# A hybrid decoder block on one core: the whole program's order written out, output weights split once, layer norms in one chain, two FFN pairs by turns, operands at multiples of 512 bytes

## The chip, the cores and the metric

The kernel runs on one core of one Trainium2 chip. The metric is the time of one execution on the device in microseconds (us). A profile of one execution records what each engine did: TensorE (PE, its weight loads as PEld), VectorE (DVE), ScalarE (ACT), GpSimd (POOL) and the sync engine (SP), which here only issues transfers (DMAs).

## The reference

One block over 16 learned tokens and 1024 tokens of width 1024, in float32. `D_FF` is 2816; `W_A = W_B = 512`.

```python
h = concat(meta, x)
xn = rms_norm(h, pre_mix_norm)
b_gate, c_gate, h_a, glu_val, glu_gate = split(xn @ w_in, 512 each)
y_a = b_gate * causal_conv3(c_gate * h_a)
g   = glu_val * sigmoid(glu_gate)
z   = causal_conv31(g) + conv_b_bias
y_b = silu(layer_norm(z, ln_b_gain, ln_b_bias))
h = h + rms_norm(concat(y_a, y_b) @ w_out, post_mix_norm)
n = rms_norm(h, pre_ffn_norm)
ff = (silu(n @ w_gate) * (n @ w_up)) @ w_down
out = (h + rms_norm(ff, post_ffn_norm))[16:]
```

## The kernel before

**Precision.** Each operand of a matmul is split into a high part (rounded to the matmul's type) and a low part (what is left); `mm3` multiplies high by high, high by low and low by high into one PSUM bank. So each product is three matmuls, and each operand needs a copy on ACT (high) and a subtraction on DVE or POOL (low).

**Input projection.** Channels lie on partitions, tokens along them. There are 20 units of 128 output channels: four each of g (gate of the gated group), v (its value), c, h and b (the short convolution group). g and v run over 1044 columns (4 of padding, 16 learned tokens, 1024 tokens) in three parts of 348, c and h over 1026 in three parts of 342, b over 1024 in two parts of 512; every part is summed over eight blocks k of the input. A unit's result takes three PSUM banks (`ps1`, two tiles, so the next unit but one waits for a unit's result to be read). Units g0 and v0 run together while the input arrives; then the sum of squares for the first norm (`ss_x`), its reciprocal root (`rsqrt_n`, on DVE), and its spread over partitions (`pb_x`, `rB`).

**Long convolution.** 31 taps over even and odd positions apart, after an identity that shares 16 taps: `ac` on the odd stream, then `ae` on the difference `d` and `ao` on the shifted difference. Each tap is one DVE instruction of 512 columns that multiplies and adds to an accumulator in a PSUM bank (`aux`, two banks). The first eight shared taps of groups 1 to 3 are done on ACT and POOL (`conv_head`). The 163 taps left for DVE were issued with low priority (`later()`).

**Layer norm.** One call for each half of the positions: sum over channels (`chunk_sum`, a matmul with `ones`), subtraction of the mean, squares, a second sum, root, spread by transposes, scale, SiLU, split. The first half was called behind unit b1, the second behind b3.

**Output projection.** Row blocks of 128 tokens in groups of three, three and two; each group runs over eight blocks of `w_out`, which each group loaded and split anew (24 splits). Then two RMS norms with the residual (`norms`), and `turn` transposes the result (`pt`, `aux` banks) into `raw`.

**FFN.** One level of Strassen's scheme in Winograd's form, seven products. For gate and up it runs over 11 pairs of blocks of `D_FF` (`Pair`), whose weights are the stationary operands (`op`) and whose seven moving operands are B11, B21, B22 and T1 to T4, sums of the transposed input's quarters (`X`). A product is 24 matmuls of 512 columns. The results are combined, split and written to DRAM (`gd`); the down projection reads them back (`a`), with `w_down`'s combinations as moving operands (`db`).

**Order.** Up to the end of the output projection a planner ordered each engine's instructions from a model of their times; from the FFN on, the program's text is the order (`manual_schedule`), and each engine takes its instructions in that order.

**Where tiles lie.** Pools are stacked from the low end of SBUF, some (`side="right"`) from the high end. `xg` holds the input's parts in the first stage and later the FFN's operands, in tiles of `lines(2 * TT)` = 2096 elements, 8384 bytes; `bp` and `rp` hold further operands of 8192 bytes, `wp` weights and operands of 4096.

Of the kernel before, what the change touches and what calls it, by code (L numbers as in the profile page):

```python
# [36 lines left out]
LOW = 2000  # L37
# [9 lines left out]
LINE = 16  # L47

# [6 lines left out]
def hybrid_block(ctx: ExitStack, tc: tile.TileContext, xT, x, w_in, w_out, w_gate, w_up, w_down, par, g_post, g_ffn, g_out, out):  # L55
# [21 lines left out]
    pr = const.tile([P, lines(NPAR)], F32, name="pr")[:, :NPAR]  # L77

    def big(name, dt=F32R, pool=None):

        if pool is None:
            return xg.tile([P, lines(2 * TT)], dt, tag="x", name=name)[:, : 2 * TT]
        return pool.tile([P, 4 * HALF], dt, tag="x", name=name)

    def row(pool, tag, name, n, dt=F32, **k):
        return pool.tile([P, lines(n)], dt, tag=tag, name=name, **k)[:, :n]
# [3 lines left out]

    def load_unit(src, name):
        ws = wp.tile([P, D], F32, tag="ws", name=f"ws_{name}", bufs=3)
        nc.sync.dma_start(ws, src)
        return ws

    def split_unit(ws, name, eng=None):
        wh = wp.tile([P, D], F32R, tag="wh", name=f"wh_{name}")
        wl = wp.tile([P, D], F32R, tag="wl", name=f"wl_{name}")
        nc.scalar.copy(wh, ws)  # L99
        (eng or nc.gpsimd).tensor_tensor(wl, ws, wh.bitcast(F32), op=ALU.subtract)  # L100
        return wh, wl

    def unit(src, name, eng=None):
        return split_unit(load_unit(src, name), name, eng)
# [47 lines left out]
    xl = [xlb[k // 2][:, k % 2, :] for k in range(KD)]

    def load_x(k):
        t = row(tp, "t", f"xs{k}", TT)[:, PAD:]
        nc.sync.dma_start(t, xT[k])
        return t

    w0 = {}
    for n in ("g0", "v0"):  # L160
        w0[n] = [wp.tile([P, D], dt, tag=tag, name=f"{tag}_in_{n}", bufs=3) for dt, tag in ((F32, "ws"), (F32R, "wh"), (F32R, "wl"))]

    def load_w0(n, m, c):
        nc.sync.dma_start(w0[n][0][:, c], units_in(m)[:, c])

    def split_w0(n, c):
        ws, wh, wl = w0[n]
        nc.scalar.copy(wh[:, c], ws[:, c])
        nc.vector.tensor_tensor(wl[:, c], ws[:, c], wh[:, c].bitcast(F32), op=ALU.subtract)

    sa = [row(gp, "g", f"sa{j}", G0 + TT)[:, G0 + PAD :] for j in range(2)]

    def split_x(k):
        h, l, t = xh[k][:, PAD:], xl[k][:, PAD:], xs[k]
        g = pr[:, O_MIX + k : O_MIX + k + 1]
        nc.scalar.activation(h, t, AF.Copy, scale=g)
        nc.vector.scalar_tensor_tensor(l, t, g, h.bitcast(F32), op0=ALU.mult, op1=ALU.subtract)

    def square_x(k):
        t = xs[k]  # L180
        if k < 2:
# [6 lines left out]
    xs = {}
    cut = [slice(0, 2 * P), slice(2 * P, D)]
    for j in range(2):  # L190
        load_w0("g0", M_G, cut[j])
        xs[j] = load_x(j)
        load_w0("v0", M_V, cut[j])
    for k in range(2, KD):
        xs[k] = load_x(k)
    for j in range(2):
        split_w0("g0", cut[j])
        split_x(j)
        split_w0("v0", cut[j])
    for k in range(KD):  # L200
        if k >= 2:
            split_x(k)
# [23 lines left out]
    sx = sm.tile([P, 16], F32, tag="sx", name="sx")  # L226
    nc.gpsimd.memset(sx, 1.0)
# [879 lines left out]
```

## Time and profile before

| | |
|---|---|
| median of three runs | 1053.48 us (1051.01 to 1054.18) |
| the profiled execution, its own time | 1052.19 us |
| its span, first to last instruction | 1050.4 us |
| granted TensorE clock, mean | 0.977 |
| busy: PE, DVE, ACT, POOL | 992.3, 782.9, 396.3, 296.7 us |
| moved by DMAs | 161.93 MB |

The page gives busy times by engine, the span in 40 slices of 26.3 us, the chain of work that ended last, and groups of instructions by line, engine and tile with the time their engine stood idle before them and what ended that. Answers from the trace give who waited for whom, busy times in any stretch, and single instructions. In a row of stages the columns are: stretch, length, busy time and count of PE, PEld, DVE, ACT and POOL, granted clock, busy share of the DMA engines, GB/s. In a row of waits they are: who, for whom, total us, times, longest.

### The profile page before, as it was taken

The page shows a single profiled execution, that of the slowest core. Times are in us where ns is not written, and L with a number is a line of the kernel's source. Part 1 is how long each engine was busy: PE and PEld are TensorE (multiplying, and loading weights), DVE is VectorE, ACT ScalarE, POOL GpSimd, SP SyncE. Part 2 cuts the span into 40 slices and gives each one's busy share as a digit, 9 for nine tenths or more (in the row PEclk, how much of TensorE's full clock was granted, in tenths as well). Part 3 has the DMA queues.
Part 4 walks back from the last instruction along what each step waited for, and adds up shares of the span by engine and source line. Part 5 has one row for each costly group of instructions (what it writes and reads, how often), then busy time and mean ns, then how long its engine had stood idle before and what let it go on. Part 6 is the DMA issues. An engine that isn't in the chain of part 4 may idle for free.

```text
span 1050.4 us, 12734 instructions
## 1 busy us (share of the span) xinstructions
PE 992.3 (94%) x4643; PEld 837.0 (80%) x4643; DVE 782.9 (75%) x1106; ACT 396.3 (38%) x640; POOL 296.7 (28%) x241
## 2 busy tenths in 40 slices
PE   8999899997799977999999999999999999999994
PEld 8998899986588765778888888888888788888773
DVE  6488778999556978788888878879877343446677
ACT  7432142333345554334425324334334233322331
POOL 4464575440000000543413313313312521221110
PEclk9999999999899989999999999999999999999997
DMA  7111111103246550254354344345217989856765
GB/s 286 44 42 37 61 41 41 47 34 100 81 161 222 190 184 5 80 182 153 125 203 157 118 166 168 121 152 183 116 63 256 330 297 379 261 180 212 267 211 211
DMA packets 59727, 161.93 MB, mean 154 GB/s; under 512 B 6289, under 2 KB 6673, under 8 KB 59665
## 3 DMA queue, kind: packets, MB, share of 16 engines
q1 hardware_dynamic: 43056, 108.35, 28.7%
q0 software_dynamic: 11088, 40.38, 12.0%
q10 hardware_dynamic: 5520, 12.40, 3.3%
q8 instruction: 36, 0.59, 0.2%
q14 instruction: 27, 0.21, 0.1%
HBM read 112.34 MB, written 48.76 MB: 153 GB/s over the span
## 4 chain that ended last, share of the span: by engine, by line
PE 61%; DVE 25%; POOL 4%; issue 4%; ACT 4%; DMA 2%; DVEq 0%; ACTq 0%; SPq 0%; POOLq 0%
PE x L108 6%; PE x L109 6%; PE x L110 6%; PE y L110 5%; PE y L109 5%; PE y L108 5%; DVE ae L300 4%; DVE ao L300 3%; PE qx L109 3%; PE qx L108 3%; PE qx L110 3%; PE po L108 3%; PE po L109 3%; PE po L110 3%; PE qy L109 3%
## 5 line engine op out<-in xcount | busy, mean ns | idle before, releaser
L544 DVE TENSOR_TENSOR op<-u,op 128x512 fp32r<-128x512 f32 x132 | 114.5, 892 | 50.4 <-ACT op L555 50.4
L555 ACT CAST op<-u 128x512 fp32r<-128x512 f32 x132 | 78.0, 617 | 154.6 <-DVE u L544 140.3
L544 DVE TENSOR_TENSOR db<-wb,db 128x512 fp32r<-128x512 f32 x77 | 54.9, 716 | 92.7 <-ACT db L912 92.4
L547 POOL TENSOR_TENSOR C<-C,C 128x512 f32<-128x512 f32 x11 | 16.9, 1539 | 344.6 <-ACT C L665 232.3
L912 ACT CAST db<-wb 128x512 fp32r<-128x512 f32 x77 | 47.2, 620 | 125.3 <-PE qx L110 59.8
L108 PE MATMUL qx<-db,a 128*128 128x512 f32 x176 | 69.4, 394 | 2.0 <-DMA a<-gdA 2.0
L109 PE MATMUL qx<-db,a 128*128 128x512 f32 x176 | 69.5, 395 | 0.4 <-DVE db L544 0.3
L110 PE MATMUL qx<-db,a 128*128 128x512 f32 x176 | 69.1, 392 | 0.0
L547 POOL TENSOR_TENSOR U<-U,U 128x512 f32<-128x512 f32 x22 | 31.6, 1435 | 114.4 <-ACT U L665 82.2
L541 DVE TENSOR_TENSOR U<-y,U 128x512 f32<-128x512 f32 x66 | 43.0, 681 | 17.6 <-PE y L110 17.6
L108 PE MATMUL qy<-db,a 128*128 128x512 f32 x132 | 51.5, 390 | 0.5 <-ACT db L912 0.5
L109 PE MATMUL qy<-db,a 128*128 128x512 f32 x132 | 51.5, 390 | 0.3 <-DVE db L544 0.3
L110 PE MATMUL qy<-db,a 128*128 128x512 f32 x132 | 51.4, 389 | 0.0
L888 POOL DMA_DIRECT2D a<-gdS x44 | 23.3, 531 | 92.5 <-PE qy L110 47.2
L100 DVE TENSOR_TENSOR wl_o<-ws_o,wh_o 128x1024 fp32r<-128x1024 f32 x24 | 30.7, 1284 | 22.5 <-ACT wh_o L99 22.3
L99 ACT CAST wh_o<-ws_o 128x1024 fp32r<-128x1024 f32 x24 | 25.2, 1052 | 49.2 <-PE po L110 36.3
L300 DVE SCALAR_TENSOR_TENSOR ae<-d,pr,ae 128x512 f32<-128x512 f32 x56 | 41.1, 749 | 0.4
L108 PEld LDWEIGHTS qx<-db,a 128*128 128x128 f32 x176 | 33.4, 190 | 9.8 <-issue 2.4
L109 PEld LDWEIGHTS qx<-db,a 128*128 128x128 f32 x176 | 33.4, 190 | 8.1 <-DVE db L544 1.2
L108 PE MATMUL y<-T2h,op 128*128 128x512 f32 x88 | 35.5, 404 | 4.1 <-DVE G L547 4.1
L110 PEld LDWEIGHTS qx<-db,a 128*128 128x128 f32 x176 | 33.5, 190 | 7.1
L108 PE MATMUL x<-B11h,op 128*128 128x512 f32 x88 | 35.4, 403 | 2.9 <-ACT op L555 2.9
(307 smaller groups left out, 3099.9 us busy)
## 6 DMA issues: line engine op xcount, KB each, us to landing
a<-gdS POOLq DMA_DIRECT2D x44, 512.0 KB, 4.7
a<-gdA POOLq DMA_DIRECT2D x33, 512.0 KB, 5.6
ws_o<-w_out_u SPq DMA_DIRECT2D x24, 512.0 KB, 3.5
u<-w_gate_u SPq DMA_DIRECT2D x22, 512.0 KB, 5.0
u<-w_up_u SPq DMA_DIRECT2D x22, 512.0 KB, 6.0
gdS<-HI SPq DMA_DIRECT2D x44, 256.0 KB, 2.3
gdA<-HI SPq DMA_DIRECT2D x33, 256.0 KB, 2.0
gdS<-GS SPq DMA_DIRECT2D x33, 256.0 KB, 2.7
```

Source lines behind the costliest of these rows:

```text
L99: nc.scalar.copy(wh, ws)
L100: (eng or nc.gpsimd).tensor_tensor(wl, ws, wh.bitcast(F32), op=ALU.subtract)
L108: nc.tensor.matmul(o, lh, rh, start=start, stop=False, skip_group_check=again)
L109: nc.tensor.matmul(o, lh, rl, start=False, stop=False, skip_group_check=again)
L110: nc.tensor.matmul(o, ll, rh, start=False, stop=stop, skip_group_check=again)
L300: nc.vector.scalar_tensor_tensor(out if i == n - 1 else acc, src[:, i : i + HALF], w(i), init if i == first else acc, op0=ALU.mult, op1=AL ...
L541: (eng or nc.vector).tensor_tensor(o, a, b, op=ALU.add)
L544: (eng or nc.vector).tensor_tensor(o, a, b, op=ALU.subtract)
L547: (eng or nc.vector).tensor_tensor(o, a, b, op=ALU.mult)
L555: nc.scalar.copy(t[:, 0, :], src)
L888: nc.gpsimd.dma_start(loads[n, j], gd[an][j])
L912: nc.scalar.copy(t[:, 0, :], b)
```

## The change

- **Order.** `manual_schedule` now begins at the top. The input projection is a loop over `UNITS`: in each round the next unit's weights are split, those of the unit after it loaded, the last unit's result is read (`after`), and a fixed number of convolution taps is issued (`LEAD_IN`). Small matmuls stand at fixed places between the blocks of a unit (`AT`).
- **Taps.** `by_turns` issues the taps of two chains alternately; chains `common(0)` and `common(3)` run alone.
- **Layer norm.** Both halves go through one chain: `ln_sum` behind the last tap, `ln_mean` behind the first block of b2, `ln_var` and `ln_spread` within c3, `ln_apply` ahead of h3. The splits of `y_b` follow b3.
- **Output weights.** `pre_out` splits each block of `w_out` once, during g0 to g1, and stores both parts in DRAM (`wo`); `load_o` loads them on POOL's queue, 18 times 1 MB, the middle group running its blocks backwards. Three blocks fit.
- **Output projection to FFN.** The transposes of a group's rows stand among the matmuls of the next group, those of 3 to 5 ahead of the last two blocks of the third. Products 1 of pairs 0 and 1 follow that group at once; the norms of rows 6 and 7 run beside them.
- **First pairs.** Pairs 0 and 1 take each product in turn (before: product 1 and 2 of both, then the rest of pair 0, then of pair 1); their splits come together later.
- **Addresses.** `xg` is a pool of its own for the FFN with tiles of 8192 bytes; a pool `fill` of 160 bytes and a wider `edge` shift the pools, so that `bp`, `xg` and `rp` start at multiples of 512 bytes. The input's parts have their own pool `xa`.
- **Smaller.** Two sums of squares go from POOL to DVE, the last group's tail of the short convolution wholly to DVE; combination 6 of a pair is done in place, part of it at product 7.

```diff
-    edge.tile([P, 8], F32, name="edge")
+    edge.tile([P, 120], F32, name="edge")
-    xg = ctx.enter_context(tc.tile_pool(name="xg", bufs=8))
+    fill = ctx.enter_context(tc.tile_pool(name="fill", bufs=1))
+    fill.tile([P, FILL], F32, name="fill")
+    bp = ctx.enter_context(tc.tile_pool(name="bp", bufs=2))
...
+    order_ = ExitStack()
+    order_.enter_context(tc.manual_schedule())
...
-        if pool is None:
-            return xg.tile([P, lines(2 * TT)], dt, tag="x", name=name)[:, : 2 * TT]
-        return pool.tile([P, 4 * HALF], dt, tag="x", name=name)
+        return (pool or xg).tile([P, 4 * HALF], dt, tag="x", name=name)
...
+    def pre_out(k):
+        load_raw_o(k + 2)
+        ws = ws_o.pop(k)
+        h, l = (yap.tile([P, D], F32R, tag="y", name=f"{c}_o{k}") for c in ("wh", "wl"))
+        nc.scalar.copy(h, ws)
+        nc.vector.tensor_tensor(l, ws, h.bitcast(F32), op=ALU.subtract)
+        for q, t in enumerate((h, l)):
+            nc.sync.dma_start(wo[k][:, q, :].bitcast(F32), t.bitcast(F32))
...
+    def conv():
+        yield from common(0)
+        yield from by_turns(even(0), odd(0))
+        yield from by_turns(common(1), common(2))
+        yield from by_turns(even(1), odd(1))
+        yield from by_turns(even(2), odd(2))
+        yield from common(3)
+        yield from by_turns(even(3), odd(3))
...
+    def after_b(a):
+        yh[a], yl[a] = (yap.tile([P, SEQ], F32R, tag="y", name=f"y{c}{a}") for c in "hl")
+        for q in range(2):
+            s = slice(q * HALF, (q + 1) * HALF)
+            nc.vector.tensor_tensor(cv[a][:, s], pu["b", a][:, q, :], cv[a][:, s], op=ALU.mult)
+        nc.scalar.copy(yh[a], cv[a])
+        nc.vector.tensor_tensor(yl[a], cv[a], yh[a].bitcast(F32), op=ALU.subtract)
...
+    def start_g():
+        spread_x()
+        nc.vector.tensor_tensor(sg[0], sg[0], rB, op=ALU.mult)
+        nc.scalar.activation(sg[0], sg[0], AF.Sigmoid)
+        pre_out(6)
+        nc.vector.tensor_tensor(sg[0], sg[0], rB, op=ALU.mult)
+        pre_out(7)
+        o3 = new_g(0)
+        nc.vector.tensor_tensor(o3.rearrange("p r n -> p n r"), vs.rearrange("p (n r) -> p n r", r=2), sg[0].rearrange("p (n r) -> p n r", r=2), op=ALU.mult)
...
+    LEAD_IN = {0: lambda: pre(range(2, 6)), 1: some(lambda: conv_head(0), lambda: tap(9)), 2: some(lambda: conv_head(1), lambda: tap(10)), 3: lambda: tap(14), 4: some(lambda: conv_head(2), lambda: tap(13)), 5: lambda: tap(14), 6: some(lambda: conv_head(3), lambda: tap(12)), 7: lambda: tap(16), 8: lambda: tap(13), 9: lambda: tap(12), 10: lambda: tap(15), 11: lambda: tap(12), 12: lambda: tap(12), 13: some(lambda: tap(40), ln_sum), 16: some(ln_apply), 17: some(gains)}
+    AT = {(0, 1): start_g, (14, 1): ln_mean, (15, 3): ln_var, (15, 7): ln_spread}
+
+    for i, u in enumerate(UNITS):
+        if i + 1 < len(UNITS):
+            split_unit(UNITS[i + 1])
+        if i + 2 < len(UNITS):
+            load_unit(UNITS[i + 2])
+        if i:
+            after[UNITS[i - 1][0]](UNITS[i - 1][1])
+        LEAD_IN.get(i, lambda: None)()
+        p = pu[u] = ps1.tile([P, 3, 512], F32, tag="p", name=f"p_{u[0]}{u[1]}")
+        for k in range(KD):
+            AT.get((i, k), lambda: None)()
+            mm_k(p, split_w[u], k, *GEO[u[0]])
...
-            w = unit(w_out[k], f"o{grp[0]}_{k}", nc.vector)
...
+    def load_o(k):
+        wu[k] = [wp.tile([P, D], F32R, tag=t, name=f"{t}_o{k}") for t in ("wh", "wl")]
+        for q in range(2):
+            nc.gpsimd.dma_start(wu[k][q], wo[k][:, q, :])
+
+    todo_o = list(range(KD)) + list(range(KD - 4, -1, -1)) + list(range(3, KD))
...
+    s1, left = group((3, 4, 5), down_, {4: turns(0, 1), 5: turns(2)})
...
+    s1, left = group((6, 7), up, {6: early})
...
+    results = {s: pairs[order[s][0]].product(order[s][1], made.pop(s)) for s in range(2)}
...
-    order = [(j, n) for n in (1, 2) for j in range(2)] + [(j, n) for j in range(2) for n in (6, 5, 7, 3, 4)]
+    order = [(j, n) for n in (1, 2, 6, 5, 7, 3, 4) for j in range(2)]
...
+    extra = {2: (load_pair(1, 1),), 3: (t2,), 4: (t1,), 6: (t3,), 8: (b22,), 9: (load_pair(2, 0),), 10: (t4,), 11: (load_pair(2, 1),)}
+    first_splits = {13: (0, "A12", "S3"), 14: (0, "S1", "A11"), 15: (0, "A22", "S2", "S4"), 16: (1, "A22", "S3", "S1"), 17: (1, "A11", "S2"), 18: (1, "A12"), 19: (1, "S4")}
```

More of the change, by code (lines that the diff above doesn't have):

```diff
@@ L152, in hybrid_block @@
[L152 to L169, printed above, removed]
@@ L188, in hybrid_block @@
[L188 to L193, printed above, removed]
-    for k in range(2, KD):
[L195 to L202, printed above, removed]
+    sx = sm.tile([P, 16], F32, tag="sx", name="sx")
+    nc.gpsimd.memset(sx, 1.0)
+    wv = pr[:, O_CB : O_CB + 4 * CB].rearrange("p (a j) -> p a j", a=4)
@@ new lines, in value @@
+    def value(a):
+        o4 = new_g(a).rearrange("p r (a n) -> p a n r", a=3)
+        for i in range(3):
+            nc.vector.tensor_tensor(o4[:, i], pu["v", a][:, i, :T3].rearrange("p (n r) -> p n r", r=2), three(sg[a])[:, i].rearrange("p (n r) -> p n r", r=2), op=ALU.mult)
+    sg[0] = row(tp, "t", "sg0", TT)
+    vs = row(tp, "t", "vs0", TT)
+    nc.scalar.copy(three(sg[0]), pu["g", 0][:, :, :T3])
+    nc.scalar.copy(three(vs), pu["v", 0][:, :, :T3])
+    zt = [bp.tile([P, 2, SEQ], F32, tag="x", name=f"z{a}") for a in range(2)]
@@ L363, in later @@
-    def later():
-        return tc.high_priority(offset=-LOW)
-    glu(0, pg0, lambda: pv0, True)
-    with later():
-        conv_head(0)
-    todo_in = [(M_G + a // 2 if a % 2 == 0 else M_V + a // 2, f"in_{'gv'[a % 2]}{a // 2}") for a in range(2, 8)]
-    todo_in += [(m + a, f"in_{c}{a}") for a in range(4) for m, c in ((M_C, "c"), (M_H, "h"), (M_B, "b"))]
-    ahead = []
-    def prepare(n):
-        while len(ahead) < n and todo_in:
-            m, name = todo_in.pop(0)
-            ahead.append((name, unit(units_in(m), name)))
@@ L406, in hybrid_block, with tap @@
+    conv_taps = conv()
+    def tap(n):
+        for i in range(n):
+            next(conv_taps, None)
+    yh, yl = [None] * 8, [None] * 8
     T0 = PAD + META
@@ new lines, in hybrid_block, with sums @@
+    after = {"g": gate, "v": value, "c": after_c, "h": after_h, "b": after_b}
+    GEO = {"g": (0, T3, 3), "v": (0, T3, 3), "c": (T0 - CA + 1, C3, 3), "h": (T0 - CA + 1, C3, 3), "b": (T0, HALF, 2)}
+    LN = [(hf, a) for hf in range(2) for a in range(4)]
+    hs_ = [slice(hf * HALF, (hf + 1) * HALF) for hf in range(2)]
+    ln = {}
+    def sums(srcs, outs):
+        for q in range(3):
+            for hf in range(2):
+                nc.vector.tensor_tensor(outs[hf], srcs(hf, 0) if q == 0 else outs[hf], srcs(hf, q + 1), op=ALU.add)
@@ new lines, in ln_sum, with ln_mean @@
+    def ln_sum():
+        ln["zs"] = [ct.tile([P, HALF], F32, tag="ct", name=f"zs{hf}") for hf in range(2)]
+        sums(lambda hf, a: z[a][:, hs_[hf]], ln["zs"])
+    def ln_mean():
+        ln["pm"] = [aux.tile([P, 512], F32, tag="a", name=f"pm{hf}") for hf in range(2)]
+        for hf in range(2):
+            nc.tensor.matmul(ln["pm"][hf], ones, ln["zs"][hf], start=True, stop=True)
+        t = [row(gp, "g", f"sq{a}", G0 + TT) for a in range(4)]
+        ln["sq"] = {(hf, a): t[a][:, hs_[hf]] for hf, a in LN}
+        for hf, a in LN:
+            nc.vector.tensor_tensor(z[a][:, hs_[hf]], z[a][:, hs_[hf]], ln["pm"][hf], op=ALU.subtract)
+            nc.scalar.activation(ln["sq"][hf, a], z[a][:, hs_[hf]], AF.Square)
+        sums(lambda hf, a: ln["sq"][hf, a], [ln["sq"][hf, 0] for hf in range(2)])
@@ L759, in hybrid_block @@
     st = ctx.enter_context(tc.tile_pool(name="st", bufs=11, reuse_waits="tile"))
-    psf = None
-    last = None
+    a_side(3)
+    for i in range(2):
+        t2_sum(i)
     def t2():
```

588 lines of the change are left out of this document (306 added, 282 removed).

## The prediction

> **What bounds the kernel now.** I read the page first (busy shares, the slices, the chain), then who TensorE waited for, then busy time by stage; for the parts the chain's pieces and single groups.
>
> ```profile
> span 1050.4 us, 12734 instructions
> PE 992.3 (94%) x4643; PEld 837.0 (80%) x4643; DVE 782.9 (75%) x1106; ACT 396.3 (38%) x640; POOL 296.7 (28%) x241
> PE   8999899997799977999999999999999999999994
> DVE  6488778999556978788888878879877343446677
> PEclk9999999999899989999999999999999999999997
> PE 61%; DVE 25%; POOL 4%; issue 4%; ACT 4%; DMA 2%; DVEq 0%; ACTq 0%; SPq 0%; POOLq 0%
> ```
>
> TensorE is 94% busy, so only its holes and its pace can give anything. The holes are in slices 10-11 and 14-15, where the granted clock drops too. The busiest helper there is VectorE, at 9 from slice 7 to 9. By stage (us, then busy time and instruction count of PE, PEld, DVE, ACT, POOL, then clock, DMA share, GB/s), and a row of the chain:
>
> ```profile
> 52.50:78.80 26.30, 26.30 (x167) 26.30 (x167) 22.29 (x22) 9.32 (x12) 17.61 (x12) 1.00 0.13 43
> ...
> 58.00:253.00 195.00, 187.11 (x1075) 177.20 (x1073) 172.66 (x224) 65.01 (x76) 99.03 (x50) 0.98 0.15 49
> 253.00:290.00 37.00, 24.65 (x94) 19.05 (x93) 23.92 (x41) 14.12 (x19) 0.00 (x0) 0.79 0.21 72
> 290.00:360.00 70.00, 70.00 (x315) 57.49 (x314) 48.78 (x91) 36.23 (x64) 0.00 (x0) 0.99 0.56 196
> 360.00:420.00 60.00, 46.43 (x198) 36.23 (x197) 48.98 (x83) 29.76 (x52) 0.00 (x0) 0.91 0.30 105
> 420.00:470.00 50.00, 46.56 (x199) 36.60 (x198) 40.69 (x49) 18.55 (x30) 23.98 (x15) 1.00 0.34 120
> 470.00:814.00 344.00, 344.00 (x1486) 278.28 (x1485) 285.81 (x357) 134.86 (x242) 98.90 (x63) 1.00 0.42 154
> 814.00:840.00 26.00, 23.97 (x99) 19.18 (x98) 9.77 (x12) 7.07 (x11) 13.72 (x16) 0.93 0.93 329
> ...
> 329.10 0.87 PE pt L501 x8
> ```
>
> The paces come from stretches without a hole: 26.30/167 = 0.1575 us for a matmul of 348 or 342 columns, 344/1486 = 0.2315 us for one of 512. Time minus count times pace is what a stage lost. From 58 to 253 us: 192 matmuls of 512 columns (the four b units) and 883 short ones make 183.5, so 11.5 us lost. From 253 to 290: 94 make 21.5, 15.5 lost. From 290 to 360: nothing. From 360 to 420: 158 of 512 and 40 transposes (eight take 0.87) make 41, 19 lost. From 420 to 470: 199 make 46, 4 lost. Around 820: 3.4 lost. Who ended the longest of these waits:
>
> ```profile
> PE po L108 <- DVE cv L428: 6.2, 1, 6.2
> PE pb_r L329 <- DVE s_ln L130: 5.7, 2, 3.3
> PE y L108 <- DVE G L547: 4.1, 1, 4.1
> PE pt L501 <- ACT raw L503: 2.2, 3, 1.7
> ```
>
> VectorE ends most of them: the convolution and the two layer norms at the change from input to output projection, then the combinations of the FFN's first products.
>
> **The change, part by part.** The reference execution is the profiled one: 1052.19 us, 1.8 more than its span and 1.3 under the median of 1053.48.
>
> *1. Input projection, convolution, layer norm.* The removed planner put taps where DVE was free; the listing now gives DVE a fixed queue, and the next unit but one of TensorE waits for each unit's `after` in that queue. Two taps by turns cost less than one chain:
>
> ```profile
> 130.45 6.67 DVE L300 SCALAR_TENSOR_TENSOR ae<-d,pr,ae 128x512 f32<-128x512 f32 x10
> 140.14 6.29 DVE L300 SCALAR_TENSOR_TENSOR ae<-d,pr,ae 128x512 f32<-128x512 f32 x8
> ...
> 32.59 1.81 PE ss_x L225 x18
> 53.54 4.28 DVE g L263
> 259.51 0.76 PE po L108
> ...
> L268 DVE TENSOR_TENSOR g<-p_in_v,sg 128x348 f32<-128x348 f32 x9 | 6.9, 762 | 0.0
> L307 DVE TENSOR_TENSOR d<-g 128x527 f32<-128x527 f32 x4 | 5.0, 1249 | 14.3 <-POOL z L295 14.3
> L313 DVE TENSOR_TENSOR g<-g 128x526 f32<-128x526 f32 x4 | 7.3, 1815 | 0.0
> L300 DVE SCALAR_TENSOR_TENSOR ac<-g,wsum,z 128x512 f32<-128x512 f32 x4 | 6.0, 1497 | 0.9 <-ACT z L291 0.9
> L300 DVE SCALAR_TENSOR_TENSOR ae<-d,pr,z 128x512 f32<-128x512 f32 x4 | 4.8, 1212 | 0.1
> L321 DVE TENSOR_TENSOR zs<-z,z 128x512 f32<-128x512 f32 x2 | 3.6, 1778 | 1.2 <-POOL z L295 1.2
> L428 DVE TENSOR_TENSOR cv<-p_in_b,cv 128x1024 f32<-128x1024 f32 x4 | 4.9, 1219 | 3.0 <-POOL cv L425 3.0
> L100 DVE TENSOR_TENSOR wl_o<-ws_o,wh_o 128x1024 fp32r<-128x1024 f32 x24 | 30.7, 1284 | 22.5 <-ACT wh_o L99 22.3
> L295 POOL TENSOR_TENSOR z<-z,ct 128x512 f32<-128x512 f32 x21 | 29.6, 1409 | 18.8 <-ACT ct L294 18.0
> ```
>
> Ten in 6.67 us is 0.667 a tap (two chains mixed), eight in 6.29 is 0.786 (one chain). The rows of 1.2 to 1.8 us have two operands in SBUF; the same shapes with an accumulator in PSUM take 0.75, and what is over that is time in which POOL was at work. The changed queue from `gate(1)` to the end of `ln_sum`:
> - 163 taps: 140 by turns, 93.4; 23 alone (`common(0)`, `common(3)`), 18.1.
> - 8 differences at the rows' means: 4 x 1.25 + 4 x 1.82 = 12.3. First taps that read `z`: 4 x 0.75 + 4 x 0.46 = 4.9 over a plain tap.
> - Three gates at 1.2, nine pieces of `value` at 0.76, two `after_h` and two `after_b` at 1.22 (the row's product): 3.6 + 6.9 + 4.9. Two `yl` with the wait for their ACT copy, which now stands directly ahead: 5.
> - `ln_sum`, six additions at 0.68 and two waits of 1.1: 6.3.
>
> That is 155.5 us. It starts at about 57 us: TensorE ends its first two units and the sums of squares at 34.4 as before (32.59 + 1.81), but ACT must first pass four `pre_out` copies, each behind a load and a buffer that a store to DRAM frees, so rB comes at about 44 and g0 at 56 (53.54 + 4.28 before). `pre_out` is 8 x 1.28 of DVE, ahead of the taps; its cover is DVE's wait for rB. So `ln_sum` ends near 212. TensorE alone would be at `ln_mean`, which stands in its queue behind block 0 of unit b2, at 34.4 + 12 x 11.34 + 2 x 11.1 + 1.4 = 194, plus up to 8 us in `spread_x`, whose third group needs the auxiliary bank that ACT frees only after those four copies. Two other queues: SP's unit loads stand behind `pre_out`'s stores, which wait for DVE, but a unit's weights are wanted two units (22 us) later: nothing. POOL's split of a unit stands behind up to seven conv-head additions, 7 x 1.41 = 9.9: `conv_head(2)` starts at about 91, the split of c0 is done some 2.4 later, at 104, when TensorE wants it: 0 to 1, within the bounds. TensorE thus waits for DVE, 10 to 18 us in all, at `ln_mean` or before it at the banks. From there: the rest of b2 9.7, c3 and h3 22.7, b3 11.1, the small matmuls 2, a wait for the root of the variance 2.5: b3 ends at about 260, 7 later than before (259.5 less the wait of 6.2). But the layer norm is done by then: 15.5 us of holes go, and `after_b(3)`'s read of PSUM costs 1.5. Sum **-7 us**. Bounds: no lock waits at all, DVE ends at 198 and TensorE's own path of 202 decides, -17; lock waits twice as long, +8. I take the measured ones, since POOL keeps its work of this stage: conv heads, tails and weight splits.
>
> *2. Output projection.* 24 splits of weights (1.28 each on DVE, a copy on ACT) become eight, done earlier; both engines are then free for the norms, but TensorE lost nothing from 290 to 360, so this gives nothing by itself. In exchange 18 loads of 1 MB, on POOL's queue, replace 24 of 0.5 MB. Each has two blocks of lead: 8.2 us with three row blocks, 5.4 in the last group.
>
> ```profile
> a<-gdS POOLq DMA_DIRECT2D x44, 512.0 KB, 4.7
> 840.00:1024.00 184.00, 182.79 (x802) 150.09 (x801) 99.40 (x165) 56.98 (x107) 35.52 (x67) 1.00 0.79 258
> ...
> GB/s 286 44 42 37 61 41 41 47 34 100 81 161 222 190 184 5 80 182 153 125 203 157 118 166 168 121 152 183 116 63 256 330 297 379 261 180 212 267 211 211
> ```
>
> Nearest row: a load of this kind lands in 4.7 us, two together some 6. The stage needs about 29 MB in 87 us, 333 GB/s; the best slice shows 379. +1 (0 to +4).
>
> *3. The change to the FFN.* `turns` now stands inside the groups. Four transposes are 0.44 us, but a bank comes back after one or two ACT copies (and a DVE subtraction for the first four row blocks), so two or three turns in a row wait: 2.0 + 2.7 + 0.7 = 5.4. The first products of pairs 0 and 1 cover the norms of row blocks 6 and 7: 10.9 us against 10.5 of DVE (root 1.7, two h 2.6, B21l 2.4, operands 1.3, the leaving tiles 1.4 and waits). Two products and two turns later, at 24 us, product 6 needs T2; DVE reaches it at about 29 (norms 4.2, operands 1.3, T sums 4.2, pair 0's combinations 4.1, G11 0.7, half of T2l 1.2): 5 to 6 lost, with a little for the clock. Later each product (5.5 us) has 4 to 5 us of DVE; the fourteen splits of pairs 0 and 1 in seven products press this to the limit, 3. With part 2, 16 lost instead of 23: **-7 us** (-15 to +1). The end (820 us, the last rows) stays.
>
> *4. Tile addresses.* In the listing an `xg` tile was 8384 bytes, of which one in eight begins at a multiple of 512; the right-hand pool began 448 past one. Now every operand tile of the FFN is 8192 bytes from such a multiple. What the place is worth shows within one product at the end, where one bank takes six blocks: four from `bp` (a multiple), the last two from `rp` (448 past):
>
> ```profile
> 1029.53 0.39 PE L110 MATMUL qx<-db,a 128*128 128x512 f32 x1
> 1031.12 0.39 PE L108 MATMUL qx<-db,a 128*128 128x512 f32 x1
> 1032.52 0.39 PE L108 MATMUL qx<-db,a 128*128 128x512 f32 x1
> ...
> 850.00:975.00 125.00, 125.00 (x553) 103.55 (x552) 60.35 (x95) 37.43 (x67) 24.27 (x46) 1.00 0.81 266
> ```
>
> Seven matmuls from 1029.53 take 0.227 each, the six from 1031.12 take 0.233. In the stage at 850 to 975, nearly all aligned, it is 125/553 = 0.226. Against 0.2315 in gate and up this is 1848 x 0.0055 = 10.2 us at most, and 1848 x 0.003 = 6 if only part of the difference is the address. I take **-8 us**.
> The Trainium skill ("TensorE: Matmul & The Clock Gate", "Wait — 56ns, not 53.3ns?") has a warm stream start every N / 2.4 GHz plus 2.5 ns, 215.7 ns at 512 columns, and names no address. By it this part gives nothing and the sum would be 1038. The trace disagrees in the size, 226 to 233, and the three rows above speak for the address.
>
> Sum: 1052.2 - 7 - 7 - 8 = **1030 us**.
>
> **Rivals.**
> - *DVE keeps pace.* If POOL and DVE collide less in the new order, part 1 gives 17: about 1020. For it: the lock waits are 14 us of the 155. Against: POOL is busy 99 of 195 us in this stage and keeps its work.
> - *Addresses don't matter.* If the last stage is quicker for another reason, part 4 gives nothing: 1038. For it: the address is no column of the profile. Against it: the three rows, of one product and one engine.
> - *Slower: the output projection becomes bound by its loads.* At 333 GB/s needed, every rate below stretches the 87 us: 258, the mean from 840 to 1024 us, gives 29/0.258 = 112, +25, so 1054; at 245, 1060. It decides below 262. For it: most slices of the last stage lie at 180 to 330. Against: these are what was asked for, and 379 was reached.
>  The Trainium skill ("SBUF — State Buffer", "SBUF: two separate sides") says that transfers issued on GpSimd's queue starve while DVE holds the shared port. The 4.7 us above, beside a DVE busy 99.4 of 184 us, don't show this.
>
> **How the numbers follow.** Forecast (1022 to 1037) 0.55; DVE keeps pace (1010 to 1021) 0.21; addresses idle 0.13; loads bind 0.07, mostly slower; all gains eaten by new waits in the FFN's start, no change, 0.04. The range 1010 to 1045 leaves out the last two. A change under 0.3% can't be told from none. Faster 0.89, same 0.04, slower 0.07.
>
> **What would show it.** Right: TensorE waits for `zs` or for banks read late by DVE between 100 and 215 us, 10 to 18 in all; b3 ends near 260 and no wait for `ybh` or the root follows; pace in gate and up 0.227; TensorE waits for T2l or pair 0's operands once, about 5 us. Wrong: a wait of `po` for loads; a pace still at 0.2315; holes over 20 us before 215.

## The result and the profile after

The changed kernel took 1062.07 us (median of five, 1059.18 to 1062.84) against 1053.48 (1050.28 to 1054.18): ratio 1.0083, interval 1.0058 to 1.0108. It is 0.8% slower, where 1030 us was forecast. The profiled execution took 1059.18 us. Of its page, the lines that answer to those of before (span, busy time by engine, the slices of PE, DVE and clock, the chain, GB/s):

```profile
span 1057.2 us, 12732 instructions
PE 986.2 (93%) x4643; PEld 839.9 (79%) x4643; DVE 773.9 (73%) x1087; ACT 378.4 (36%) x616; POOL 296.3 (28%) x267
PE   9599998879999797998999999999999899999994
DVE  6689999997414558789888888888878343446667
PEclk9799998989999999999999999999999999999998
GB/s 304 301 216 41 41 42 60 20 20 61 254 163 316 183 184 74 1 122 177 219 130 149 160 170 148 130 209 117 142 100 169 384 309 376 270 183 204 268 215 209
PE 60%; DVE 26%; DMA 5%; ACT 4%; issue 4%; POOL 1%; SPq 0%; DVEq 0%; ACTq 0%; POOLq 0%
```

Counted from 1, PE has a 5 in slice 2, where it had a 9, and the clock a 7 there; 301 GB/s flow in that slice and 216 in the next, where it was 44 and 42 before. The holes of slices 10 and 11 are gone, as forecast; those that stand ahead of them (slices 7 to 9) come with a DVE that is at 9 from slice 4 to 9. In the chain DMA has 5% instead of 2%. Who TensorE waited for:

```profile
PE pb_x L286 <- ACT rB L289: 10.6, 1, 10.6
PE p_h L109 <- DVE cv L412: 7.3, 2, 3.9
PE pm L435 <- DVE zs L426: 6.2, 1, 6.2
PE x L109 <- ACT U L677: 5.3, 2, 4.1
PE y L109 <- DVE G L595: 4.4, 1, 4.4
PE po L110 <- DMA wl_o<-wo: 3.9, 4, 1.8
PE po L109 <- DMA wh_o<-wo: 3.5, 1, 3.5
```

By stage, with the columns of the prediction's rows: the first 58 us of before, then of after; the convolution; the third group of the output projection; and 280 us of gate and up without a hole, before and after.

```profile
0.00:58.00 58.00, 53.93 (x336) 52.77 (x337) 34.29 (x35) 30.78 (x34) 25.59 (x31) 1.00 0.42 157
...
0.00:58.00 58.00, 43.69 (x240) 42.09 (x241) 38.52 (x45) 36.38 (x39) 11.23 (x23) 0.85 0.82 312
58.00:253.00 195.00, 181.51 (x1042) 172.59 (x1041) 186.57 (x223) 54.74 (x66) 106.89 (x55) 0.96 0.15 51
...
355.00:375.00 20.00, 13.70 (x49) 9.88 (x48) 9.80 (x21) 3.46 (x6) 4.86 (x10) 0.83 0.96 333
...
520.00:800.00 280.00, 280.00 (x1210) 226.45 (x1209) 233.79 (x292) 109.33 (x196) 80.99 (x51) 1.00 0.39 143
...
520.00:800.00 280.00, 280.00 (x1237) 231.92 (x1236) 236.44 (x297) 112.46 (x202) 84.25 (x55) 1.00 0.40 146
```

Four readings. In its first 58 us TensorE ran 240 matmuls instead of 336, at a clock of 0.85. In the convolution DVE was busy 186.57 of 195 us (172.66 before). In the third group 49 matmuls ran in 20 us, at 333 GB/s and a clock of 0.83. And in gate and up a matmul now takes 280/1237 = 226 ns instead of 280/1210 = 231: that part came, in full.

Where the first hole is made stands in ACT's time line (start, duration, instruction, in brackets the idle time before it and what ended it):

```profile
37.25 1.05 ACT L256 CAST wh_o<-ws_o 128x1024 fp32r<-128x1024 f32 x1
39.63 1.04 ACT L256 CAST wh_o<-ws_o 128x1024 fp32r<-128x1024 f32 x1 [1.33 <-DMA wo<-wh_o]
43.77 1.04 ACT L256 CAST wh_o<-ws_o 128x1024 fp32r<-128x1024 f32 x1 [3.09 <-DMA ws_o<-w_out_u]
48.13 1.04 ACT L256 CAST wh_o<-ws_o 128x1024 fp32r<-128x1024 f32 x1 [3.31 <-DMA ws_o<-w_out_u]
49.08 0.66 ACT L289 ACTIVATE rB<-pb_x 128x16 f32<-128x16 f32 x2
```

Four copies of output weights, the last three each behind a store or a load, take 12 us; only then comes rB, for which TensorE waits (`pb_x`) and behind which DVE's taps stand.

DVE's first instructions of a chain, all with two operands in SBUF: one group of before that the prediction doesn't show, the groups of after, then those once in order of time, with POOL's at the same time:

```profile
L300 DVE SCALAR_TENSOR_TENSOR ao<-g,pr,z 128x512 f32<-128x512 f32 x4 | 3.0, 753 | 0.0
...
L341 DVE SCALAR_TENSOR_TENSOR ae<-d,pr,z 128x512 f32<-128x512 f32 x4 | 9.3, 2337 | 0.0
L341 DVE SCALAR_TENSOR_TENSOR ao<-g,pr,z 128x512 f32<-128x512 f32 x4 | 9.3, 2335 | 0.0
L353 DVE TENSOR_TENSOR g<-g 128x526 f32<-128x526 f32 x4 | 8.9, 2221 | 0.2
...
L352 DVE TENSOR_TENSOR d<-g 128x527 f32<-128x527 f32 x4 | 6.9, 1718 | 0.0
...
152.50 2.09 DVE L352 TENSOR_TENSOR d<-g 128x527 f32<-128x527 f32 x1
154.63 2.79 DVE L353 TENSOR_TENSOR g<-g 128x526 f32<-128x526 f32 x1
157.34 2.89 DVE L341 SCALAR_TENSOR_TENSOR ae<-d,pr,z 128x512 f32<-128x512 f32 x1
160.14 2.88 DVE L341 SCALAR_TENSOR_TENSOR ao<-g,pr,z 128x512 f32<-128x512 f32 x1
162.94 0.74 DVE L341 SCALAR_TENSOR_TENSOR ae<-d,pr,ae 128x512 f32<-128x512 f32 x1
...
151.60 5.25 POOL L405 TENSOR_TENSOR cv<-cv,u 128x1024 f32<-128x1024 f32 x2 [7.29 <-ACT u L404]
156.93 2.75 POOL L406 TENSOR_TENSOR cv<-cv,rB 128x1024 f32<-128x1024 f32 x1
159.63 2.84 POOL L155 TENSOR_TENSOR wl_h<-ws_h,wh_h 128x1024 fp32r<-128x1024 f32 x1
```

Before, the same four groups had means of 1.21, 0.75, 1.82 and 1.25 us; now 2.34, 2.34, 2.22 and 1.72. That is 1.13 + 1.59 + 0.40 + 0.47 = 3.6 more for each of four channel groups, 14 in all. With the four `ac` that begin a chain these are 20 instructions. Before, 7 of them met POOL and took over 1.6 us, the others 0.69 to 0.76; after, 17 took 1.6 or more. The hand-written order puts the four in a row, and POOL is at work at that moment: on additions of 512 columns in the first two channel groups, where a DVE instruction that meets one takes 1.6 to 1.8 us, and on instructions of 1024 in the last two. There the two engines take turns, 2.8 us a turn, and each of DVE's ends 0.55 us behind POOL's: 160.23 after 159.68, 163.02 after 162.47.

### The profile page after: what moved, and what is told of

It is laid out like the page before. It is cut to its first block, busy times and chain, and to the rows that moved or that the text cites. A ratio compares the mean times of both kernels' runs of the same rounds, so it can differ in the third digit from the quotient of the medians.

```text
span 1057.2 us, 12732 instructions
## 1 busy us (share of the span) xinstructions
PE 986.2 (93%) x4643; PEld 839.9 (79%) x4643; DVE 773.9 (73%) x1087; ACT 378.4 (36%) x616; POOL 296.3 (28%) x267
## 4 chain that ended last, share of the span: by engine, by line
PE 60%; DVE 26%; DMA 5%; ACT 4%; issue 4%; POOL 1%; SPq 0%; DVEq 0%; ACTq 0%; POOLq 0%
PE x L109 6%; PE x L111 6%; PE x L110 6%; PE y L109 5%; PE y L110 5%; PE y L111 5%; DVE ao L341 4%; DVE ae L341 4%; PE qx L110 3%; PE qx L109 3%; PE qx L111 3%; DVE ac L341 3%; PE qy L110 2%; PE qy L111 2%; PE qy L109 2%
## 5 line engine op out<-in xcount | busy, mean ns | idle before, releaser
L592 DVE TENSOR_TENSOR op<-u,op 128x512 fp32r<-128x512 f32 x154 | 142.9, 955 | 61.6 <-ACT op L605 61.6
L605 ACT CAST op<-u 128x512 fp32r<-128x512 f32 x154 | 90.7, 618 | 163.6 <-DVE u L592 153.6
L109 PEld LDWEIGHTS qx<-db,a 128*128 128x128 f32 x176 | 33.0, 188 | 10.8 <-ACT U L705 3.6
L592 DVE TENSOR_TENSOR u<-u,u 128x512 f32<-128x512 f32 x44 | 39.9, 907 | 0.8
L109 PE MATMUL x<-B21h,op 128*128 128x512 f32 x88 | 35.0, 398 | 5.3 <-ACT U L677 5.3
L109 PE MATMUL p_h<-xh,wh_h 128*128 128x342 f32 x96 | 32.8, 341 | 7.3 <-DVE cv L412 7.3
L110 PEld LDWEIGHTS qx<-db,a 128*128 128x128 f32 x176 | 33.0, 188 | 7.9 <-DVE db L592 1.2
L341 DVE SCALAR_TENSOR_TENSOR ao<-g,pr,ao 128x512 f32<-128x512 f32 x52 | 38.8, 747 | 0.0
```

Source lines behind the costliest of these rows:

```text
L109: nc.tensor.matmul(o, lh, rh, start=start, stop=False, skip_group_check=again)
L110: nc.tensor.matmul(o, lh, rl, start=False, stop=False, skip_group_check=again)
L341: nc.vector.scalar_tensor_tensor(out if i == n - 1 else acc, src[:, i : i + HALF], w(i), init if i == first else acc, op0=ALU.mult, op1=AL ...
L592: (eng or nc.vector).tensor_tensor(o, a, b, op=ALU.subtract)
L605: nc.scalar.copy(t[:, 0, :], src)
```

## The experiments

Each kernel was timed beside the kernel before. What an edit gave is the difference of its ratio from the changed kernel's 1.0083, times 1051 us; such a difference carries about 3 us of uncertainty.

**1. The addresses: 64 bytes off (e_shift).**

```diff
-FILL = 40
+FILL = 56
-    edge.tile([P, 120], F32, name="edge")
+    edge.tile([P, 136], F32, name="edge")
```

> The changed kernel with every FFN operand tile moved 64 bytes off a multiple of 512 (fill 160 to 224 bytes, edge 480 to 544); nothing else differs. Address theory: the pace in gate and up goes from 0.2265 us a matmul back to about 0.231 to 0.232, 1848 matmuls, so 8 to 11 us slower than the changed kernel (about 1070). Rival, the new order or the quieter engines gave the pace: no change in pace, 1060 to 1062.

1070.46 us, ratio 1.0176 (1.0158 to 1.0193): 9.8 slower than the changed kernel.

```profile
520.00:800.00 280.00, 280.00 (x1216) 228.20 (x1216) 232.13 (x294) 109.13 (x197) 78.83 (x52) 1.00 0.40 147
```

1216 matmuls instead of 1237 in the same 280 us, 230 ns each: the place of the tiles is the cause of the better pace.

**2. 256 bytes off (e_256).** 40 becomes 104, 120 becomes 184.

> The changed kernel with every operand of the FFN 256 bytes behind a multiple of 512 (40 becomes 104, 120 becomes 184). If 512 bytes is the step that counts: as with 64 bytes, 1068 to 1071, ratio 1.016 to 1.019. If a multiple of 256 is enough, it stays at 1062, ratio 1.007 to 1.010. If each 64 bytes have their share, in between, 1065 to 1067.

1062.1 us, ratio 1.0113 (1.0092 to 1.0134), an interval that overlaps that of the changed kernel.

```profile
520.00:800.00 280.00, 280.00 (x1237) 231.86 (x1236) 236.58 (x295) 112.46 (x202) 85.42 (x55) 1.00 0.39 144
```

1237 again: with all operands 256 bytes past a multiple of 512 the pace is the same, so a multiple of 256 is enough. The time alone would have left this open; the pace doesn't.

**3. One pool of the kernel before, aligned (e_before_rp).**

```diff
-    edge.tile([P, 8], F32, name="edge")
+    edge.tile([P, 120], F32, name="edge")
```

> The kernel before with one number changed: the tile at the right end is 480 bytes instead of 32, so that the pool rp begins at a multiple of 512 bytes and not 448 past one. In each of the 11 pairs 64 of the 168 matmuls read from it (T2, the low part of T1, the high parts of T3 and B22), 704 in all. My theory (a moving operand off a multiple of 512 costs 5 to 5.5 ns per matmul of 512 columns): 3.5 to 3.9 us faster, ratio 0.9962 to 0.9967, and the start-to-start of T2's matmuls falls to 227 ns. Rival (it's not the place of the operand but what else the change did to gate and up): ratio 0.999 to 1.001.

1049.51 us against 1050.98, ratio 0.9992 (0.998 to 1.0005): the rival's time. The pace says why (mean time from one matmul's start to the next's, worked out from all starts in the trace; gaps over 260 ns left out):

| moving operand, ns | before | this kernel | changed | 256 off | 64 off |
|---|---|---|---|---|---|
| T2, high part | 233.4 | 226.9 | 226.9 | 226.9 | 233.4 |
| B22, high part | 233.3 | 229.3 | 226.6 | 226.6 | 232.1 |
| T1, low part | 230.8 | 235.0 | 226.8 | 226.8 | 230.5 |
| T3, high part | 231.0 | 232.7 | 226.6 | 226.6 | 232.5 |
| all of gate and up | 231.8 | 230.9 | 226.8 | 226.8 | 230.5 |

T2, whose two parts both lie in `rp`, gains 6.5 ns. B22's high part, T1's low part and T3's high part are aligned now too, but their other halves lie in `xg` and are not: B22 got 4.0 ns faster, T1 4.2 and T3 1.7 slower. High and low alternate in the stream, and only a pair with both aligned reached 227. My price for each matmul by itself was wrong; why one aligned half helps in one pair and costs in another is open.

The output projection shows one thing more. Its moving operands, `wh_o` and `wl_o`, lie in `wp`, which no run moved. This run moved `yh` and `yl`, half of its stationary operands, onto multiples of 512 bytes: their three kinds of matmul went from 227.9 to 230.7 ns down to 227.2 to 227.5, while those of `ybh` and `ybl`, which stayed where they were, kept between 229.8 and 231.3. In run 1 all four moved off, and the stage's mean went from 227.4 in the changed kernel to 231.2 ns. So the place of the stationary operand counts as well.

**4. POOL's long instructions in two halves (e_half).** The weight splits, the gate's product and the tails of the short convolution, all in the convolution stage:

```diff
-        nc.gpsimd.tensor_tensor(wl, raw_w[u], wh.bitcast(F32), op=ALU.subtract)
+        for q in range(2):
+            c = slice(q * 512, (q + 1) * 512)
+            nc.gpsimd.tensor_tensor(wl[:, c], raw_w[u][:, c], wh[:, c].bitcast(F32), op=ALU.subtract)
...
```

> The changed kernel with POOL's additions, products and subtractions of the convolution stage (weight splits, gates, tails) cut into two instructions of half the columns. Lock theory: a DVE instruction with two operands in SBUF waits for the POOL instruction under way, now 1.0 to 1.4 us instead of 2 to 2.9, so the 20 differences and first taps lose about half of their 26 us of waits; zs ends 10 to 13 us earlier (229 to about 217) and the total falls by 8 to 12. Rival, the two engines share bandwidth and the waits follow the bytes: zs stays within 3 us, total within 3. Second rival, DVE's delay is not what holds TensorE: zs earlier but the total unchanged.

1049.85 us, ratio 0.9987 (0.9975 to 0.9998): 10 us gained. Of DVE's instructions only the four of the last channel group's tail, which run there, were halved too; all others are as they were.

```profile
L348 DVE SCALAR_TENSOR_TENSOR ao<-g,pr,z 128x512 f32<-128x512 f32 x4 | 7.2, 1792 | 0.0
L348 DVE SCALAR_TENSOR_TENSOR ae<-d,pr,z 128x512 f32<-128x512 f32 x4 | 7.1, 1787 | 0.0
L360 DVE TENSOR_TENSOR g<-g 128x526 f32<-128x526 f32 x4 | 6.7, 1683 | 0.1
...
L359 DVE TENSOR_TENSOR d<-g 128x527 f32<-128x527 f32 x4 | 4.6, 1160 | 0.0
```

Each of the four kinds is 0.54 to 0.56 us shorter in the mean, and with the four `ac` the 20 instructions take 30.2 us instead of 41.2. That is the 11 us by which `zs` ends earlier (219.0 instead of 229.9). All of it comes from places where POOL's instruction was halved. In the first two channel groups, beside additions of 512 columns that are the same in both kernels, `ae` and `ao` take 1.8 us in both. In the last two they go from 2.89 to

```profile
153.03 1.78 DVE L348 SCALAR_TENSOR_TENSOR ae<-d,pr,z 128x512 f32<-128x512 f32 x1
```

so that the wait, which is what goes beyond 0.75, falls from 2.1 to 1.0 us. The wait is what is left of POOL's instruction, in a row the whole of it, and halving the instruction halves the wait; both rivals are out. This is what the Trainium skill ("SBUF — State Buffer", "SBUF: two separate sides") states: the port pair of VectorE and GpSimd is held by whichever instruction got it, to its end, if VectorE's has two inputs in SBUF and GpSimd's reads SBUF. The traces agree, with 0.68 to 0.77 us for a tap whose accumulator lies in PSUM, at any time, and up to 2.89 for one that reads two SBUF tiles.

**5. The splits behind the taps, on DVE (e_spread).**

```diff
-    LEAD_IN = {0: lambda: pre(range(2, 6)), 1: some(lambda: conv_head(0), lambda: tap(9)), ...
+    LEAD_IN = {1: some(lambda: conv_head(0), lambda: tap(9), lambda: pre((2, 3))), 2: ... pre((4, 5)), 3: ... pre((6, 7)), ...
```

> The changed kernel with the splits of output weights 2 to 7 moved behind the taps of the next three units (two each), so that ACT copies rB at once. Hole theory: TensorE's 10.6 us wait in pb_x and its slow clock go, and the total falls by all of it, 12 to 13 us. Queue theory (DVE paces the stage): the hole goes, but zs moves only by the time DVE stood idle between 36 and 62 us, about 11, and the waits of p_h and pm grow instead: total 8 to 11 lower, p_h plus pm at 14 to 18 us instead of 13.5.

1056.7 us, ratio 1.0051 (1.0035 to 1.0066): only 3.4 gained, less than either theory had. No trace of this run shows where the rest went; the next run bears on it.

**6. The same, one split a unit, low parts on POOL (e_lead).** As in 5, but for units 1 to 7 and with

```diff
-        nc.vector.tensor_tensor(l, ws, h.bitcast(F32), op=ALU.subtract)
+        for c in (slice(0, 512), slice(512, 1024)):
+            (nc.vector if k < 2 else nc.gpsimd).tensor_tensor(l[:, c], ws[:, c], h[:, c].bitcast(F32), op=ALU.subtract)
```

> Splits of output weights 2 to 7 stand behind the taps of units 1 to 7, one per unit, and their low parts go from VectorE to POOL in two halves. My theory (the hole at 30 to 42 us is made by the ACT copies of these splits standing ahead of rB, and it is passed on to the end because VectorE's queue of taps starts late by as much): the wait of pb_x for rB falls from 10.6 to under 2, the first tap is issued at about 58 us instead of 65.6, zs ends at 220 to 223 instead of 229, and the time is 1053 to 1056 against 1062 for the changed kernel, ratio to the kernel before 1.000 to 1.004. Rival (what the start gives is lost to the port: 14 us more of POOL beside the taps): the first taps of a chain rise above 2.4 us, zs stays at 228 to 230, the waits for cv and zs grow from 13.5 to 22 and more, and the time is 1059 to 1062, ratio above 1.0055.

1047.58 us, ratio 0.9973 (0.9955 to 0.9991): 11.6 gained, more than the 6 to 9 expected.

```profile
36.71 1.53 ACT L290 ACTIVATE rB<-pb_x 128x16 f32<-128x16 f32 x3
...
0.00:58.00 58.00, 54.51 (x334) 53.65 (x335) 43.80 (x50) 34.23 (x37) 20.95 (x28) 0.97 0.61 230
...
L427 DVE TENSOR_TENSOR zs<-zs,z x4: 693/694/696, 212.6 to 214.4; 128x512 f32<-128x512 f32 x4
```

The same row of the changed kernel:

```profile
L426 DVE TENSOR_TENSOR zs<-zs,z x4: 689/690/690, 227.4 to 229.2; 128x512 f32<-128x512 f32 x4
```

rB comes at 36.7 instead of 49.1, 334 matmuls run in the first 58 us, and `zs`, the end of DVE's queue, is done by 215 instead of 230. The first tap starts 14.8 us earlier (50.8 instead of 65.6), and `zs` ends 14.8 us earlier: the whole delay of the start had gone through the taps to the end of the stage. Six splits left on DVE (5) would cost its queue 6 x 1.28 = 7.7 us, which fits the 8 between the two runs; that is worked out, not seen in a trace.

**7. No loads in the third group (e_noload).**

```diff
-                mm3(pm[i][q], yh[k][:, c], yl[k][:, c], wu[k][0][:, d], wu[k][1][:, d], ...)
+                w = wu[k % 3 if grp[0] == 6 else k]
+                mm3(pm[i][q], yh[k][:, c], yl[k][:, c], w[0][:, d], w[1][:, d], ...)
```

> The changed kernel with the third group of the output projection (rows 6 and 7) using the three weight blocks that are there, in place of loading blocks 3 to 7 again: its five loads of 1 MB and their waits are gone, its result is another one. Load theory: the waits for wh_o and wl_o at 360 to 375 us (6.3) and the low clock behind them go, total 8 to 10 lower. Rival, the FFN's first products wait for DVE anyway and take the time back: group 3 ends earlier but the total falls by under 4.

1052.56 us, ratio 1.0002 (0.9986 to 1.0018): 8.5 gained, as the load theory had it, and TensorE no longer waits for `wh_o` or `wl_o`.

**8. The residual's transfers behind the loads (e_late).**

```diff
+        for i in (3, 4, 5):
+            nc.sync.dma_start(hd[i], h35[i])
+        hs.update({i: residual_x(i) for i in (6, 7)})
```

These lines stand in `early`; the store in `norms` and the loads ahead of the group are gone.

> The stores of the residual rows 3 to 5 and the loads of rows 6 and 7 (2.5 MB) are issued behind the last load of w_out of the third group, at about 375 us, instead of at 357 to 367. My theory (these transfers collide with the loads of w_out): po's waits for wh_o and wl_o fall from 6.3 to under 2 together and the clock in that stretch stays at 1.0; the time is 1054 to 1057, nearly that of the kernel that loads nothing in the third group (ratio 1.0002). Rival (1 MB for each 2.7 us of matmuls is too much by itself): the waits stay at 4 and more, and the time is 1059 to 1062.

1056.2 us, ratio 1.0049 (1.0031 to 1.0068): 3.6 gained. The third group in both, first with the transfers moved, then without loads:

```profile
355.00:375.00 20.00, 18.04 (x89) 14.09 (x88) 12.20 (x23) 8.21 (x15) 4.22 (x8) 1.00 1.05 346
...
355.00:375.00 20.00, 18.54 (x94) 15.27 (x93) 13.27 (x26) 9.60 (x18) 0.00 (x0) 1.00 0.42 157
```

89 matmuls at a clock of 1.0, nearly the 94 without any load, and at 346 GB/s no less was moved than the 333 of the changed kernel. TensorE's waits for `wh_o` and `wl_o` fall from 6.3 us to 0.7. In the changed kernel the transfers of three of the five blocks, issued beside the residual's, took 9 to 14 us to land; here those of all five take 4 to 6. So the loads of `w_out` alone don't bind; the 2.5 MB that ran beside them did. Of the 9 us by which the first FFN product started earlier in this trace, 2 were lost again before product 6 and 1 more by the end (span 1051.4 against 1057.2). The median gains less than this trace, and less than run 7; where that goes isn't shown.

**9. Combination 6 of pair 1 back on POOL (e_pool6).** In `a_side`, product 6, `eng = nc.gpsimd if self.j == 1 else nc.vector`.

> The two additions of combination 6 of pair 1 are on POOL again, as they were before the change (four instructions of about 0.7 us leave VectorE). My theory (VectorE is what is late at 490 us, y waits for G 4.4 us there and x for U 3.6): those waits fall by 2 to 4 in sum and the time is 1058 to 1060. Rival (the waits come from the splits that stand ahead in VectorE's queue, or POOL's own slower additions make operand 6 late): nothing falls, 1061 to 1064.

1059.85 us, ratio 1.0089 (1.0058 to 1.012): no gain in the ratio. The waits did fall, as my theory had it: y for G, 4.4 us, is gone and x for U takes 3.7 instead of 5.3, while y for T2h takes 3.6 instead of 1.1. The time lies in the theory's range too, but the kernel before was also faster beside this run (1050.65). A gain under 3 us can't be told from none here, so this stays unsettled.

**10. Three repairs together (e_best): 4, 6 and 8.**

> Three repairs in one: POOL's long instructions of the convolution stage in two halves, the splits of output weights 2 to 7 behind the taps with their low parts on POOL, and the stores and loads of the residual behind the loads of w_out. If the three causes stand beside each other: 12 by the halves, 7 by the start and 6 by the loads off 1062, so 1035 to 1040, faster than the kernel before by 1.0 to 1.5%. If VectorE's queue of taps bounds the first stage whatever the start does: 1042 to 1046.

1030.82 us, ratio 0.9819 (0.979 to 0.9848). The three gains, 10 + 11.6 + 3.6 = 25, came to 27.7 together, more than the sum expected: the three causes stand beside each other. It beats both kernels. That it lands near the forecast's 1030 is partly chance, since the FFN's first products still wait and the addresses gave more than forecast. TensorE's largest wait is then

```profile
PE pm L443 <- DVE zs L434: 7.5, 1, 7.5
```

**11. Two more (e_best2).** Besides the three:

```diff
-    AT = {(0, 1): start_g, (14, 1): ln_mean, (15, 3): ln_var, (15, 7): ln_spread}
+    AT = {(0, 1): start_g, (14, 7): ln_mean, (15, 7): ln_var, (16, 3): ln_spread, (16, 4): ln_apply}
...
+                eng = nc.gpsimd if self.j < 2 else nc.vector
```
and `t2` directly behind the sums of T2, ahead of the operands of product 6.

> The kernel with three repairs (1030.8) and two more: the layer norm's small matmuls later (mean in front of the last block of b2 instead of the second, root behind h's unit of group 3 has begun its last block, spread and scaling within h3), and T2's split ahead of the operands of product 6, whose additions for pairs 0 and 1 go to POOL. My theory (TensorE waits at pm only because it stands six blocks too early for VectorE, and at product 6 because T2h stands behind copies that wait for VectorE): pm's wait of 7.5 goes without a new one at b3's end, the waits for T2h, T2l and G fall from 6 to under 2; 1030.8 - 8 - 4 = 1017 to 1021. Rival (VectorE's work is what is missing, and the wait only moves): the same 8 us turn up at the layer norm's end or at the first operands of the output projection, and the same 4 at operand 6; 1028 to 1032.

1022.84 us, ratio 0.9735 (0.9711 to 0.976): 8 to 9 more, the fastest kernel of the study, close to the theory's time. The first of the two did it: the wait at `pm` is gone, with 1.8 us new at `pst`, and the output projection starts 7 us earlier. The second gave nothing; the wait moved from T2 to the operand of product 6 (2.9 and 1.5 us). DVE's rows beside POOL's additions:

```profile
372.54 1.79 DVE L599 TENSOR_TENSOR raw<-raw,raw 128x512 f32<-128x512 f32 x1
374.43 1.60 DVE L599 TENSOR_TENSOR T2r<-raw,raw 128x512 f32<-128x512 f32 x1
377.15 3.44 DVE L599 TENSOR_TENSOR T2l<-T2r,T2h 128x1024 fp32r<-128x1024 f32 x2 [1.12 <-ACT T2h L822]
380.52 3.43 DVE L599 TENSOR_TENSOR op<-u,op 128x512 fp32r<-128x512 f32 x2
```

**12. The additions on DVE again (e_best3).** The line with `eng` is taken out.

> As the kernel with five repairs (1022.8), but the additions of product 6 for pairs 0 and 1 are on VectorE again; T2's split stays ahead of them. My theory (beside POOL's additions VectorE's instructions with two operands in SBUF waited for the port: raw 1.79, T2r 1.60, T2l 1.7 each, op 1.7 each instead of 0.68 to 1.2, some 5 us in all, more than the 2.8 us of additions that had left VectorE): these rows go back to 0.69 and 1.2, the waits of y for op (4.4 us) fall to 1 to 2, and the time is 1019 to 1022. Rival (the operands of product 6 are late because their weights are loaded late, at 372 us): no change, 1022 to 1024, or the additions' own 2.8 us come back: 1025.

1027.31 us, ratio 0.9759 (0.9738 to 0.9781): not the 1 to 4 us gained that I expected. It is 2.5 us slower by the ratio, and the intervals of the two runs overlap.

```profile
372.52 0.69 DVE L599 TENSOR_TENSOR raw<-raw,raw 128x512 f32<-128x512 f32 x1
373.31 0.69 DVE L599 TENSOR_TENSOR T2r<-raw,raw 128x512 f32<-128x512 f32 x1
375.12 2.36 DVE L599 TENSOR_TENSOR T2l<-T2r,T2h 128x1024 fp32r<-128x1024 f32 x2 [1.12 <-ACT T2h L821]
...
PE y L109 <- DVE G L602: 6.9, 1, 6.9
```

The rows went back to 0.69, as I said, but the additions stand in DVE's queue with their copies on ACT between them, and y waits 6.9 us, where it waited 4.4 in run 11. In these two traces waiting for the port is the cheaper of the two; the times can't tell them apart.

## Why the prediction was wrong

Two steps failed most: part 1 took DVE's waits for the port from the old order, and part 2 took the loads of the third group at a mean rate. Laid against the forecast, the output projection starts 19 us late (279.1 instead of some 260), the third group loses 10 instead of 1, the first FFN products lose some 6 more than I gave them, and the addresses give 2 more. That is 34 less 2, for the 29 that the profiled execution lies above 1030; the few microseconds left over weren't traced. Of the 19, DVE's queue from `gate(1)` on starts 5.5 us late (62.5 instead of 57), takes 12 more (167.4 instead of 155.5), and what follows takes 1 more. The rival of the loads comes nearest in time (1054 to 1060), but the loads cost 10 us and not its 25 to 30.

- **Part 1, the start: mechanism named, cover wrong.** I let the four `pre_out` copies put rB at 44 and TensorE lose up to 8. rB came at 49 to 51; TensorE waited 10.6 us for it, up to 49.3, and with the low clock ran 96 matmuls fewer in its first 58 us than before, 15 us at 0.1575. I had also called the cover of `pre_out` "DVE's wait for rB", which it was itself making: four of its copies stand ahead of rB. Run 6 shows what the step cost in all, 11.6 us, of which I had given some.
- **Part 1, the waits for the port: the term that was mis-sized.** "At the rows' means" took the means of another order for this one. The planner had scattered these instructions, and 7 of 20 met POOL; the listing sets four of them in a row, 17 of 20 met it, and 14 us came on top. It is the "twice as long, +8" that I had as a bound and thrown out because POOL keeps its work; the same work of POOL costs more when DVE's instructions meet it. Run 4 shows the wait and its length; that the order is what doubled it is read from the two traces, and no run gave DVE its old order back.
- **Part 1, the rest, was right:** TensorE waits at `zs` and at the banks, 13.5 us in all (10 to 18 forecast), and no wait for the root follows. The size is partly luck: it is a difference of two ends, and both came late, DVE's by 18 us (230 instead of 212) and TensorE's by 14 (without these waits 216 instead of at most 202).
- **Part 2: a mean where a burst counted.** 29 MB in 87 us was compared with 379 GB/s. Over the whole stage (279 to 387 us) 237 GB/s were moved, but the stores of three residual rows and two loads fall among the last five loads of `w_out`. The slower rival saw the place but not the mechanism; runs 7 and 8 show it.
- **Part 3: sizes.** The first products lost 20 us (387 to 500 us, clock included) instead of 14: 8.6 around T2 (413 to 430 us) instead of 5 to 6, and about 9 at the operands of pairs 0 and 1 instead of 3. Runs 9 and 12 show that moving additions between POOL and DVE doesn't settle it; why these waits are longer stays open.
- **Part 4 had the cause right and its rule wrong:** 5.0 ns over 1848 matmuls and 2.5 over the output projection's, 10.2 us against 8. The rule of the Trainium skill that names no address ("TensorE: Matmul & The Clock Gate", "Wait — 56ns, not 53.3ns?") would have given nothing here; runs 1 to 3 measure 226.8 against 230.5 to 231.8. That it takes 512 bytes was wrong, so was the price by single operands, and the stationary operands, which count too (run 3), had no term.
- **A miscount without weight:** counted from 1, VectorE's 9s ahead of the first hole stand in slices 8 to 10 and the second hole in 15 and 16, one later than I wrote; the stages in us are right.

## What to carry to other kernels

When an order is rewritten, take durations from the order that will run, not from the one that ran: an instruction that can wait for a shared port costs what its neighbours on the other engine make of it, and four in a row wait four times. Work put "in a gap" must be checked for what it does to the event that ends the gap, and a stage's rate of transfers for its worst few microseconds, not its mean. Before moving work away from a busy engine, cut the other engine's instructions in half: here that alone gave 10 us.

## What the runs showed of the hardware

- In gate and up a matmul of 512 columns starts every 226.8 ns in the mean if its moving operands, the high and the low in turn, all lie at multiples of 512 bytes or all 256 past one, and every 230.5 if all lie 64 bytes off. With one of a pair aligned it went either way (B22 233.3 to 229.3, T1 230.8 to 235.0).
- The stationary operand's place counts too: 227.4 against 231.2 ns in the output projection, with its moving operands unmoved (changed kernel and run 1).
- VectorE's wait for the port lasts to the end of POOL's instruction: beside 1024 columns a tap with two operands in SBUF took 2.89 us, beside halves of 512 it took 1.78, alone 0.75.
- Over 58 us with a hole of 10.6 us TensorE's granted clock was 0.85 in the mean (0.97 in run 6, without that hole), and over 20 us with waits of 6.3 us in all it was 0.83 (1.00 in run 8, without them).
